# A hybrid encoder block on one core: each engine's order drawn by the other timing model

## The chip, the core and the metric

The kernel runs on one core of a Trainium2 chip. The core has five engines, each of which works off its own list of instructions in the order in which the list is written: PE (TensorE, matmuls, with PEld for its weight loads), DVE (VectorE), ACT (ScalarE), POOL (GpSimd) and SP (SyncE, which here does nothing but issue transfers). An instruction that needs another engine's or a transfer's result carries a wait, and while it waits everything behind it in its list waits too. The metric is the device time of one execution in microseconds (us).

## The reference

The reference is one layer of an encoder with 2048 tokens of width 1024, in float32. What it computes, cut to its core:

```python
xn = rmsnorm(h, norm_mix_g)
q, k, v, u, y = split(xn @ w_in)              # 3 x 512 attention, 2 x 512 recurrence
q, k = rope(q), rope(k)
attn = dilated_mixture_attention(q, k, v)     # 8 heads x 64, three (window, dilation) patterns, merged by lse
uc = centred_depthwise_conv(u, conv_w, conv_b)
rec = bidirectional_rglru(uc, gates...) * gelu(y)   # forward and backward linear recurrence
h = h + concat([attn, rec]) @ w_out
h = h + memory_cross_attention(rmsnorm(h), rmsnorm(mem))    # 4 heads x 128, 256 memory tokens
h = h + square(relu(rmsnorm(h) @ w_mlp_in)) @ w_mlp_out     # hidden width 4096
return rmsnorm(h, norm_final_g)
```

## The kernel before

Every product of the large matrices is made in three matmuls (`mm3`, lines 120 to 123): each operand is split into a high part, rounded by ACT (a copy into a rounded type), and a low part, the difference, made by DVE or POOL. So behind every load stands an ACT instruction and a subtraction, and the matmuls wait for those.

The work runs in stages that follow one another in time:

- 0 to about 700 us: the combined input projection, unit by unit (`block`, line 582). For a unit the raw weights come through a ring of three buffers (`wraw`, line 232: load, line 233; high part on ACT, line 234; low part on POOL or DVE, line 235). The products land in a rotation of matmul banks and are finished by kind: u and y (`uy_unit`), v (`v_unit`, line 458 scales the product and frees the bank), q and k (`qk_unit`, which calls `rope`, lines 378 to 395: six DVE instructions, then the high part at 392, the low part at 393 and their stores at 394 and 395, each from one of two buffers). Beside the projections a generator (`lru`, line 470) runs the recurrence in 16 chunks of 512 tokens by 128 channels, one step of it after each piece of projection. A chunk has a convolution (`conv`, lines 496 to 501) and for both directions two gate matmuls into the two banks named "a" (lines 519 and 522), which ACT reads and frees with a tanh (lines 520 and 523); then further functions on ACT (lines 524 to 526, the square root at 533) and scans on DVE (lines 538 and 543). ACT loads a function table where the next function isn't in the present one.
- at about 700 us a seam: the last q unit, and the first head's loads (`load_head`, line 178), among them the v tiles (lines 193 to 202) on SP's queue.
- 760 to about 1200 us: the attention, in units of two tiles with scores, transposes and values written two units apart (line 866 on), the recurrence's half of the output projection as filler.
- 1200 to about 1700 us: the other half of the output projection and the cross-attention.
- 1700 to about 2230 us: the MLP's first product (`InPair`, line 1131), 32 passes of seven products of block sums and differences.
- 2230 us to the end: the second product (`Part`, line 1259, and the loop at 1437), 16 passes of seven products; its sums and differences (lines 1257, 1282 to 1294) and its low parts (line 1305) are shared between DVE and POOL, and DVE adds each product to the accumulators (line 1459).

Nearly all transfers are issued by SP, from one queue, in the order of its list; POOL issues the loads of q and k.

What sets the order. The Python code is not the order of the lists. It is run once and writes down the instructions; the framework then plans them. It keeps a clock for every engine and a model of what each instruction and each transfer takes, and at each moment an engine takes, among the instructions whose inputs the model says are there, the one with the earliest place in the written order. The order in which the plan takes them is the engine's list. Tiles that share a ring get their buffers in the same pass. The written order is moved by hand in a few places: `tc.high_priority` (lines 628 and 1365) gives a stretch an earlier place, and `tc.issue_after` (lines 639, 666, 868, 1400) puts instructions behind a named one whatever the plan says. These hold under either model. The waits that keep the result right are worked out from the data, not from the plan's times, so the times decide only the order.

## Time and profile before

| what | value |
|---|---|
| median of 3 runs | 2923.38 us (2919.47 to 2930.01) |
| the profiled execution's own time | 2928.47 us |
| its span, first to last instruction | 2926.6 us |
| mean granted clock of PE | 0.942 |
| busy: PE, DVE, ACT, POOL | 2590.2, 2010.9, 1277.1, 1256.2 us |
| moved by transfers | 372.00 MB, 127 GB/s over the span |

The profile is of one execution. A busy time is the time in which an engine runs an instruction; in the rows of groups and of the order of time, what stands in brackets or behind the last bar is the idle time of the engine just before, and what ended it. "PE m L121 <- DVE v L458" reads: PE's matmul of line 121 into a bank named m waited until DVE's instruction of line 458 had run on a tile named v. SPq is SP's queue of issues. PEclk is the share of full speed that the throttle granted to PE.

### The profile page before, as it was taken

Reading aid. Unit: us, or ns where it says so; the run is one execution under the profiler, and the core shown is the slowest. Engines: PE = TensorE matmul, PEld = TensorE weight load, DVE = VectorE, ACT = ScalarE, POOL = GpSimd, SP = SyncE. Lnnn points to the kernel's source line nnn. Section 1 sums busy time; section 2 is a strip of 40 time slices with the busy share of each in tenths; the row PEclk is TensorE's granted clock in tenths of the full one; section 3 lists DMA queues with packets and bytes.
Section 4 is the critical chain, followed back from the end, with each engine's and each line's share of the span. In section 5 each row is a group of like instructions: output and inputs, shape, how many; then the busy total and the mean of one; then the engine's idle time right before and its main releaser. Section 6 shows DMA issues by size and latency. Waiting matters only on the chain. (4 is left out here: it accounts for less than half of the span.)

```text
span 2926.6 us, 39992 instructions
## 1 busy us (share of the span) xinstructions
PE 2590.2 (89%) x14074; PEld 2196.7 (75%) x14074; DVE 2010.9 (69%) x3361; ACT 1277.1 (44%) x2349; POOL 1256.2 (43%) x888
## 2 busy tenths in 40 slices
PE   7897776776779989897997899989999999999997
PEld 6776665665679989786885788868887777778776
DVE  6644656765678878634567754474447999999997
ACT  5527355461646656623444233343333333334342
POOL 2222120203334434343124655555655776666652
PEclk9998888888789999898998999999999999999999
DMA  7452334426667876554344433343336222122213
GB/s 194 144 133 82 105 81 145 123 96 156 180 170 189 216 181 155 187 160 123 101 136 142 143 109 112 109 140 112 112 108 216 86 73 87 65 87 80 72 58 115
DMA packets 267352, 372.00 MB, mean 127 GB/s; under 512 B 93072, under 2 KB 139792, under 8 KB 264080
## 3 DMA queue, kind: packets, MB, share of 16 engines
q1 hardware_dynamic: 262864, 342.19, 38.3%
q0 software_dynamic: 4288, 27.27, 4.0%
q8 instruction: 111, 1.82, 0.3%
q14 instruction: 89, 0.73, 0.1%
HBM read 254.73 MB, written 114.65 MB: 126 GB/s over the span
## 5 line engine op out<-in xcount | busy, mean ns | idle before, releaser
L1304 ACT ACTIVATE c<-raw 128x512 fp32r<-128x512 f32 x162 | 102.2, 632 | 272.2 <-PE m L122 147.5
L1155 POOL TENSOR_TENSOR wl<-wr,wh 128x512 fp32r<-128x512 f32 x96 | 145.4, 1515 | 150.2 <-ACT wh L1154 150.1
L1154 ACT ACTIVATE wh<-wr 128x512 fp32r<-128x512 f32 x128 | 80.9, 632 | 287.4 <-PE m L122 153.9
L763 ACT ACTIVATE sm<-sm,obp 128x256 f32<-128x256 f32 (+1 forms) x384 | 161.9, 468 | 48.1 <-DVE obp L760 41.4
L1155 DVE TENSOR_TENSOR wl<-ws,wh 128x512 fp32r<-128x512 f32 x96 | 81.0, 843 | 130.0 <-ACT wh L1154 124.7
L235 POOL TENSOR_TENSOR wl<-wraw,wh 128x512 fp32r<-128x512 f32 x48 | 71.0, 1484 | 198.0 <-ACT wh L234 195.5
L760 DVE CUSTOM_DVE_ANT_0 sm<-a,msk 128x256 f32<-128x256 f32 (+1 forms) x384 | 131.2, 371 | 31.9 <-PE a L757 28.2
L121 PE MATMUL m<-xh,wh 128*128 128x512 f32 x328 | 132.6, 404 | 19.6 <-ACT xh L329 8.1
L775 ACT ACTIVATE ph<-b 128x512 f16<-128x512 f32 (+1 forms) x192 | 100.4, 523 | 94.1 <-PE b L772 88.6
L1176 DVE TENSOR_TENSOR c<-m,c 128x512 f32<-128x512 f32 x64 | 44.2, 690 | 139.9 <-PE m L123 137.9
L776 DVE SCALAR_TENSOR_TENSOR pl<-b,ph 128x512 f16<-128x512 f32 (+1 forms) x192 | 114.6, 598 | 26.5 <-ACT ph L775 22.7
L122 PE MATMUL m<-xl,wh 128*128 128x512 f32 x328 | 131.8, 402 | 0.3 <-DVE xl L330 0.3
L772 PE MATMUL b<-prt,sm 128*128 128x128 f32 x640 | 108.5, 285 | 26.2 <-DVE pl L776 17.2
L123 PE MATMUL m<-xh,wl 128*128 128x512 f32 x328 | 130.9, 399 | 0.0
L1305 POOL TENSOR_TENSOR wh<-raw,c 128x512 fp32r<-128x512 f32 x58 | 93.6, 1631 | 78.1 <-ACT c L1304 66.1
L702 POOL TENSOR_SCALAR kc<-kh 128x1024 fp32r<-128x1024 f32 x32 | 68.6, 2144 | 129.6 <-PE a L756 117.4
L756 PE MATMUL a<-kc,qb 128*128 128x256 f32 x256 | 108.7, 425 | 6.0 <-DVE obp L760 5.9
L1177 DVE SCALAR_TENSOR_TENSOR c<-c 128x512 f32<-128x512 f32 x96 | 111.6, 1163 | 1.0
L234 ACT ACTIVATE wh<-wraw 128x512 fp32r<-128x512 f32 x96 | 57.8, 623 | 118.2 <-DMA wraw<-in_w_in 70.0
L1154 ACT ACTIVATE wh<-ws 128x512 fp32r<-128x512 f32 x96 | 60.5, 630 | 109.6 <-PE m L122 107.9
L123 PE MATMUL m<-t3h,wl 128*128 128x512 f32 x276 | 107.6, 390 | 0.4 <-POOL wl L1155 0.3
L121 PE MATMUL m<-wh,xh 128*128 128x256 f32 x192 | 62.1, 328 | 51.3 <-DVE v L458 33.9
(556 smaller groups left out, 9789.6 us busy)
## 6 DMA issues: line engine op xcount, KB each, us to landing
wr<-in_w_m SPq DMA_DIRECT2D x64, 512.0 KB
hid_d<-c SPq DMA_DIRECT2D x128, 256.0 KB
wraw<-in_w_in SPq DMA_DIRECT2D x80, 256.0 KB
raw<-in_w_m SPq DMA_DIRECT2D x33, 512.0 KB
rawt<-hid_d SPq DMA_DIRECT2D x26, 512.0 KB
t0h<-hid_d SPq DMA_DIRECT2D x26, 512.0 KB
o_d<-obp SPq DMA_DIRECT2D x16, 528.0 KB
obr<-o_d SPq DMA_DIRECT2D x16, 528.0 KB
```

The source lines that it names most:

```text
L121: pe.matmul(o, ah, bh, start=start, stop=False, **kw)
L122: pe.matmul(o, ah, bl, start=False, stop=False, **kw)
L123: pe.matmul(o, al, bh, start=False, stop=stop, **kw)
L756: pe.matmul(so, q0, kh[:, w0:w0 + 256], start=True, stop=False)
L760: dve.tensor_tensor_reduce(out=sm, in0=sps[:, 256 * z + o0:256 * z + o0 + kw], in1=msk[:, m:m + kw], op0=ALU.add, op1=ALU.min, scale=1.0, ...
L763: exps.append(act.activation(sm, sm, AF.Exp, scale=-1.0, bias=self.obp[:, oc, 65:66]))
L772: pe.transpose(pt[:, c0:c0 + 128], self.sm[:, z, 128 * g:128 * g + 128], idt)
L776: dve.scalar_tensor_tensor(self.pl[:, :w], pt[:, :w], 1024.0, self.ph[:, :w], op0=ALU.mult, op1=ALU.subtract)
L1154: act.activation(h, self.a[n], AF.Copy)
L1155: last[n % 2] = (pool if n % 2 else dve).tensor_tensor(l, self.a[n], f32(h), op=ALU.subtract).ins
L1177: dve.scalar_tensor_tensor(z, z if n < 6 else o, 0.0, z, op0=ALU.max, op1=ALU.mult)
L1304: act.activation(h[-1], tk, AF.Copy)
```

## The change

One argument is given to the framework's context. Its planner works as before, by the same rule and from the same written order, but takes its times from its other timing model, the one that follows each transfer event by event (the issue, the queue, the transfer on its engines, the notice of its end) rather than pricing it as a whole. No line that computes, loads or stores is touched.

```diff
-    with tile.TileContext(nc) as tc:
+    with tile.TileContext(nc, schedule_with_timeline_sim=True) as tc:
         hybrid_block(tc, *args)
```

## The prediction

> **What bounds the kernel now.** I read the page first, then the busy time in eight stretches that follow the kernel's parts, then the waits of PE stretch by stretch, and last the order of time around the longest waits. The forecast is made against the profiled execution, whose span is 2926.6 us and whose own time is 2928.47 us (1.9 us lie around the span). That is 5.1 us above the median of the runs, 2923.38 us.
>
> ```profile
> span 2926.6 us, 39992 instructions
> ...
> PE 2590.2 (89%) x14074; PEld 2196.7 (75%) x14074; DVE 2010.9 (69%) x3361; ACT 1277.1 (44%) x2349; POOL 1256.2 (43%) x888
> ```
>
> ```profile
> core 0: us, PE busy (x) PEld busy (x) DVE busy (x) ACT busy (x) POOL busy (x), PEclk, DMA share, GB/s
> 0.00:300.00 300.00, 253.00 (x1218) 211.53 (x1218) 159.54 (x253) 151.81 (x244) 67.08 (x76) 0.93 0.50 139
> 300.00:700.00 400.00, 305.35 (x1490) 258.67 (x1489) 261.98 (x336) 190.73 (x276) 73.23 (x70) 0.86 0.40 111
> 700.00:760.00 60.00, 19.17 (x113) 16.83 (x112) 26.00 (x58) 13.17 (x24) 7.16 (x8) 0.63 0.65 179
> 760.00:1200.00 440.00, 397.60 (x4021) 387.54 (x4020) 346.09 (x1201) 275.45 (x694) 176.86 (x119) 0.94 0.69 179
> ...
> 1700.00:2230.00 530.00, 519.88 (x2276) 428.37 (x2275) 284.03 (x332) 188.60 (x332) 302.72 (x198) 0.99 0.34 117
> 2230.00:2927.00 697.00, 650.51 (x2907) 529.81 (x2906) 641.95 (x726) 267.77 (x382) 429.21 (x239) 0.99 0.27 92
> ```
>
> The reader is to see three different kernels here. From 1700 to 2230 us (the MLP's first product) PE is busy 519.88 of 530 us at a granted clock of 0.99: there is nothing to win, and DVE (284 us) and ACT (189 us) have so much slack that a different order of theirs costs nothing either. From 2230 us on (the second product) PE and DVE are both nearly full, 651 and 642 of 697 us. And from 0 to 760 us (projections and recurrence) PE stands idle for 760 − 253.00 − 305.35 − 19.17 = 182 us, at a clock down to 0.86 and 0.63. That is where order can matter most. The waits of PE there, 300 to 700 us:
>
> ```profile
> PE a L121 <- ACT tr L520: 42.6, 5, 11.8
> PE m L121 <- DVE v L458: 24.8, 7, 7.0
> PE m L121 <- ACT wh L234: 17.4, 2, 9.3
> PE a L121 <- ACT ti L523: 8.1, 3, 4.0
> ```
>
> The first and the last are the gate matmuls of the recurrence: 42.6 + 8.1 = 50.7 us. They need one of the two "a" banks, which ACT frees by its tanh (lines 520, 523). What ACT did at the longest of them, in order of time (the rows of ACT, then PE's):
>
> ```profile
> 344.84 0.63 ACT L234 ACTIVATE wh<-wraw 128x512 fp32r<-128x512 f32 x1 [13.03 <-DMA wraw<-in_w_in]
> 345.49 1.28 ACT L520 ACT_TABLE_LOAD   x1
> 346.78 0.69 ACT L520 ACTIVATE tr<-a,gbh 128x512 f32<-128x512 f32 x1
> ...
> 483.95 0.72 ACT L329 ACTIVATE xh<-xr,prt 128x512 fp32r<-128x512 f32 x1 [9.38 <-DMA xr<-in_xT]
> 484.57 0.67 ACT L520 ACTIVATE tr<-a,gbh 128x512 f32<-128x512 f32 x1
> ```
>
> ```profile
> 347.52 0.80 PE L121 MATMUL a<-uh,gh 128*128 128x512 f32 x1 [10.97 <-ACT tr L520]
> ...
> 485.30 0.79 PE L121 MATMUL a<-uh,gh 128*128 128x512 f32 x1 [6.02 <-ACT tr L520]
> ...
> 512.61 0.80 PE L121 MATMUL a<-uh,gh 128*128 128x512 f32 x1 [11.76 <-ACT tr L520]
> ```
>
> ACT stood 13.03 and 9.38 us before an instruction whose load had not landed, and the tanh that PE wanted was the next one in its list and was run as soon as ACT was past it. An engine works off its list in the order written there, so a load that lands later than the planner believed holds up whatever is listed behind its reader. The plan had the load landed by then; on the chip it was not.
>
> **The change, part by part.** No instruction is added or removed: the 14074 matmuls, 3361 DVE and 2349 ACT instructions stay, with the same tiles and the same bytes. What moves is the order in each list: at each moment of the plan an engine takes, among the instructions whose inputs the plan has ready, the earliest written one, and the plan's moments now come from a model that follows each transfer.
>
> *Gate waits, 300 to 700 us.* If the plan knows that the weights land late, it lists the tanh ahead of the split that waits for them. Of the waits quoted, 10.97 and 6.02 us are plainly of this kind (17 us); at 512.61 a wait for a load is only part. Bounds: 0 (the new model has the loads land as early as the old) and 50.7 us (all such waits go). I take half, −25 us, since 17 are shown and part of the 11.76 is alike.
>
> *The clock behind those waits.* The matmul after a wait takes 0.80 us in the rows above. The stretch ran at a mean clock of 0.86, the attention stretch, with fewer waits, at 0.94. If half the gate waits go and the clock rises to 0.89, the 305.35 us of work become 305.35 × 0.86 / 0.89 = 295: −10 us. Bounds: 0, and 305.35 × (1 − 0.86 / 0.94) = 26 us.
>
> *What is late next.* The ring of raw weights has three buffers, filled by SP and emptied by ACT's split (line 234) and the subtraction behind it on POOL or DVE (line 235):
>
> ```profile
> SPq L233 <- POOL wl L235: 33.5, 11, 7.4
> ```
>
> SP issues the next load only when a buffer is read out (33.5 us of waits, 11 times). A split that is listed later, behind the tanh, frees its buffer later, and SP's queue, on which every other load and store of this stretch stands behind that wait, issues later. PE waited twice for finished weights, 17.4 us together; I count one more such wait, 17.4 / 2 = +9 us. Bounds: 0, and one for each of the six longest gate waits, 6 × 8.7 = 52 us.
>
> *The waits for v.* (24.8 us) PE has all matmul banks full there; only an earlier DVE instruction helps, and the plan prices DVE much the same. I take 0; bounds −12 (half) and +12.
>
> *The seam to attention, 700 to 760 us.* PE waits 31.15 us there for the last rotary pair:
>
> ```profile
> 705.59 5.52 SPq L194 DMA_DIRECT2D v<-v_d  x1
> ...
> 712.46 6.50 SPq L394 DMA_DIRECT2D k_d<-rh  x1
> 719.05 7.23 SPq L395 DMA_DIRECT2D k_d<-rl  x1
> ```
>
> ```profile
> 732.00 0.69 DVE L393 SCALAR_TENSOR_TENSOR rl<-t,rh 128x512 fp32r<-128x512 f32 x1 [17.97 <-DMA k_d<-rl]
> ...
> 739.12 0.58 PE L756 MATMUL a<-kh,qb 128*128 128x256 f32 x1 [31.15 <-DVE t L385]
> ```
>
> SP's issues of one load and two stores took 5.52 + 6.50 + 7.23 = 19 us, and DVE waited 17.97 us for a store to give its buffer back. The v load was issued before those stores were ready, and a planner that takes what is ready will issue it first again. I take 0; bounds −18 (DVE's wait goes) and +10.
>
> *Attention (760 to 1200) and what lies between.* PE is at 398 of 440 us. 0, bounds ±10.
>
> *The second MLP product.* The planner's order there can differ only in how far ahead DVE and POOL split. 0; the bound follows with the rival that it makes.
>
> Sum: −25 − 10 + 9 = −26 us, so 2928.5 − 26 = 2902.5 for a profiled run, and **2897 us** on the median's scale (2923.4 − 26).
>
> **The rivals.** *DVE beside POOL (slower).* In the second product, 13 passes of 40 us; DVE's busy time on line 1305, then on line 1257, then two forms of line 1305 (min/median/max ns):
>
> ```profile
> 2270.00:2790.00 520.00, 235.91 (x142) 203.64 (x128) 1.00 0.24 80
> ...
> 2270.00:2790.00 520.00, 45.36 (x26) 126.25 (x46) 1.00 0.24 80
> ```
>
> ```profile
> L1305 DVE TENSOR_TENSOR wh<-raw,c x23: 675/691/1357, 2252.0 to 2767.5; 128x512 fp32r<-128x512 f32 x23
> ...
> L1305 DVE TENSOR_TENSOR t1l<-t1h,t1l x8: 1209/2434/2831, 2277.6 to 2787.0; 128x1024 fp32r<-128x1024 f32 x8
> ```
>
> The same subtraction takes 1209 ns or 2831 ns, by what runs beside it; POOL is busy over 60% of this stretch. A pass now has (235.91 + 45.36) / 13 = 21.6 us of such work on DVE. If the redrawn order puts all of it beside POOL, nine of 1024 elements at 2434 ns and four of 512 at 1357 ns give 27.3 us, 5.7 more. DVE's spare time is (697 − 641.95) / 16 = 3.4 us a pass; from that point on the pass grows: 5.7 − 3.4 = 2.3 us, times 16 passes +37 us. Without the gain ahead of it that is 2960 us. For it: DVE is already what PE waits for there. Against it: a lucky overlap is as likely as an unlucky one, and the bound the other way is the same size. The Trainium skill (GPSIMD Engine Reference, section 1, Specifications) says that POOL shares its SBUF interfaces with VectorE and that an instruction of DVE with two SBUF inputs contends for them; lines 1305 and 1257 are of that kind, and the trace agrees, 1209 against 2831 ns.
>
> *Waits change places (no difference).* Each gate wait that goes is followed by a wait for weights, since the ring is paced by how long a load takes: −50.7 + 52, the clock as it was, 2923 us. The same time results if the change doesn't do what it says, because the two models agree on the order wherever it matters.
>
> *A recurrence that comes late (slower).* Passing the waiting readers lets projections run ahead of the recurrence, and its rest is run at the seam, with PE at the 0.63 clock and 19 of 60 us busy. Its 16 chunks fill at least the 400 us from 300 to 700, 25 us a chunk; left over at the seam, a chunk has nothing beside it. From about one chunk on this outweighs the gain; for two, 2897 + 2 × 25 = 2947 us. For it: PE's list would then hold fewer gates in a stretch where they are what it waits for. Against it: the recurrence is written ahead of the projections that it runs beside, and so comes first whenever it is ready.
>
> ```profile
> L533 ACT ACT_TABLE_LOAD x13 | 16.7, 1283 | 0.2
> ```
>
> A new order of ACT also draws the table loads anew: ten more would be 13 us of ACT at the row's 1283 ns, in a stretch (300 to 700) where ACT is busy 191 of 400 us, so I leave them out. The Trainium skill (ScalarE: Activation LUTs, section What ACT_TABLE_LOAD costs) prices a switch at about 2.66 us with the drain; by it ten more would be 27 us, an estimate, where the trace shows 1.29 us from a load's start (345.49) to the next instruction's (346.78).
>
> **How the numbers follow.** The forecast has 0.50, waits that change places 0.15, DVE beside POOL 0.18, the late recurrence 0.17. A measurement of this kernel can tell about 0.3%, 9 us. Faster 0.50, same 0.15, slower 0.35. The forecast's own range goes from −60 (gate waits and clock at two thirds of their bounds, 51, and 9 us from the rest) to −9: 2863 to 2914 us. The range for the time reaches 15 us further down, for the seam's 18, and up past both slower rivals, with the larger one grown by a half (2923 + 56): 2848 to 2980 us.
>
> **What would show it.** Right: ACT's waits for the raw weights and for x shrink and no tanh stands behind them; gate waits from 300 to 700 us fall from 51 to about 25 us, the clock there rises to 0.89, the stretch ends 25 us sooner, and everything from 1700 us on keeps its length. Wrong: PE's waits for finished weights take their place; the second product's passes leave 40 us; or the seam grows. If the time lies over 2932 us, the idea that the plan's early loads were the fault is wrong, or its gain was lost in the second product.

## The result, and the profile after

The changed kernel takes 3012.84 us (median of 4 runs, 3003.89 to 3026.26) against 2923.89 us for the kernel before on the same chip: the ratio is 1.0317, 95% interval 1.0289 to 1.0346. It is 3.2% **slower**. The forecast was 2897 us, and the range ended at 2980: wrong in sign and outside the range. The profiled execution took 3003.89 us, its span is 3002.1, 75.5 us more than before.

The head of the page of the changed kernel (PE's busy time, share of the span and instructions, then the other engines):

```profile
span 3002.1 us, 40037 instructions
...
PE 2613.6 (87%) x14074; PEld 2216.9 (74%) x14074; DVE 1984.8 (66%) x3361; ACT 1283.7 (43%) x2354; POOL 1281.4 (43%) x888
```

The work is the same: 14074 matmuls, 3361 DVE and 888 POOL instructions (ACT has 5 more, table loads). Of the 75.5 us, PE is busy 23.4 longer (2613.6 − 2590.2) with the same matmuls, and idle 52.1 longer.

For a fair comparison I cut both traces at the same work rather than at the same times: at the first instruction of a line that opens a stage (756 the first scores, 923 the other half of the output projection, 1171 the MLP's first product, 1459 the second, 1483 the end). The busy time in those stretches, before:

```profile
0.00:739.10 739.10, 566.33 (x2740) 476.46 (x2740) 435.82 (x607) 345.06 (x524) 147.47 (x153) 0.88 0.46 126
739.10:1204.40 465.30, 408.80 (x4096) 398.11 (x4096) 362.19 (x1257) 287.63 (x715) 178.61 (x121) 0.92 0.68 180
1204.40:1607.40 403.00, 360.87 (x1720) 296.50 (x1720) 221.07 (x374) 161.67 (x353) 136.77 (x144) 0.94 0.47 141
1607.40:2250.80 643.40, 620.25 (x2675) 508.32 (x2676) 370.61 (x415) 221.62 (x388) 379.11 (x240) 0.98 0.36 123
2250.80:2868.10 617.30, 591.35 (x2577) 479.68 (x2575) 579.12 (x636) 244.77 (x338) 400.10 (x212) 1.00 0.25 84
2868.10:2926.60 58.50, 42.62 (x269) 37.68 (x268) 42.07 (x77) 16.33 (x34) 14.12 (x19) 0.89 0.36 126
```

And of the changed kernel:

```profile
0.00:786.20 786.20, 576.91 (x2740) 485.95 (x2740) 430.20 (x609) 355.12 (x529) 155.14 (x153) 0.85 0.41 119
786.20:1269.40 483.20, 420.07 (x4097) 406.24 (x4097) 350.32 (x1240) 285.72 (x713) 180.17 (x119) 0.90 0.65 174
1269.40:1690.50 421.10, 365.85 (x1725) 298.11 (x1721) 214.91 (x378) 159.47 (x350) 135.98 (x144) 0.93 0.42 133
1690.50:2345.30 654.80, 624.49 (x2677) 508.41 (x2678) 379.53 (x427) 224.70 (x391) 370.09 (x241) 0.97 0.36 123
2345.30:2937.50 592.20, 580.57 (x2556) 478.04 (x2555) 560.12 (x629) 241.13 (x338) 422.62 (x210) 1.00 0.25 84
2937.50:3002.10 64.60, 45.72 (x289) 40.11 (x287) 49.70 (x86) 17.56 (x37) 17.43 (x23) 0.87 0.37 131
```

The matmuls of a stretch agree to within 5, but for the last two: 21 fewer in the second product, 20 more in the tail behind it. At 0.23 us a matmul some 5 us of the second product's 25.1 have only moved across that cut.

The reader is to see that the loss isn't in one place. The first stage grows by 47.1 us, attention by 17.9, the middle by 18.1, the first product by 11.4; the second product *shrinks* by 25.1 and the tail grows by 6.1. In each stage that grows the granted clock is 0.01 to 0.03 lower, and the same matmuls take longer (566.33 to 576.91 us for 2740 of them in the first stage): where PE stands idle longer, its matmuls also run at a lower clock. The Trainium skill (TensorE: Matmul & The Clock Gate, section HAM oscillation) says that idle gaps of PE over some 3.4 us bring the throttle back; the rows agree in the direction, and no row here shows that threshold.

PE's waits of the changed kernel from 300 to 700 us, the stretch that the prediction argued from:

```profile
PE m L121 <- ACT wh L234: 35.0, 3, 15.8
PE a L121 <- ACT tr L520: 18.7, 5, 7.5
PE a L121 <- ACT ti L523: 18.4, 5, 5.2
PE m L121 <- DVE t L385: 17.1, 2, 14.4
PE b L121 <- DVE t L386: 11.9, 1, 11.9
PE m L121 <- DVE v L458: 7.2, 3, 4.7
PE b L121 <- DVE v L458: 5.0, 1, 5.0
PE b L121 <- DVE t L385: 3.0, 1, 3.0
```

```profile
300.00:700.00 400.00, 283.49 (x1348) 239.40 (x1347) 254.65 (x328) 202.61 (x283) 70.75 (x66) 0.82 0.37 106
```

The gate waits did fall (50.7 to 18.7 + 18.4 = 37.1 us) and so did those for v (26.3 to 12.2; the prediction's row has 24.8 of the 26.3, the bank named b has the rest), but the waits for finished weights doubled (17.4 to 35.0), and 32.0 us of waits for the banks that the rotary step reads (17.1 + 11.9 + 3.0, lines 385 and 386) stand where there were none. In the same 400 us PE did 1348 matmuls instead of 1490.

### The profile page after: what moved, and what is told of

Same layout as the page of the kernel before. It is cut to its first block, busy times and chain, and to the rows that moved or that the text cites. A ratio compares the mean times of both kernels' runs of the same rounds, so it can differ in the third digit from the quotient of the medians.

```text
span 3002.1 us, 40037 instructions
## 1 busy us (share of the span) xinstructions
PE 2613.6 (87%) x14074; PEld 2216.9 (74%) x14074; DVE 1984.8 (66%) x3361; ACT 1283.7 (43%) x2354; POOL 1281.4 (43%) x888
## 4 chain that ended last, share of the span: by engine, by line
PE 55%; DMA 19%; DVE 15%; ACT 5%; issue 4%; POOL 2%; SPq 0%; DVEq 0%; ACTq 0%; POOLq 0%
PE m L121 13%; PE m L122 13%; PE m L123 13%; DMA obr<-o_d 3%; DMA k_d<-rl 2%; PE a L123 2%; PE a L121 2%; PE a L122 2%; DMA h_d<-h 2%; PE a L756 2%; DMA wraw<-in_w_in 2%; DMA q_d<-rl 1%; PE b L772 1%; PE b L122 1%; PE b L123 1%
## 5 line engine op out<-in xcount | busy, mean ns | idle before, releaser
L1155 POOL TENSOR_TENSOR wl<-wr,wh 128x512 fp32r<-128x512 f32 x96 | 132.3, 1379 | 168.0 <-ACT wh L1154 168.0
L1155 DVE TENSOR_TENSOR wl<-ws,wh 128x512 fp32r<-128x512 f32 x96 | 97.2, 1014 | 116.3 <-ACT wh L1154 99.5
L760 DVE CUSTOM_DVE_ANT_0 sm<-a,msk 128x256 f32<-128x256 f32 (+1 forms) x384 | 129.5, 374 | 66.8 <-PE b L772 64.1
L121 PE MATMUL m<-xh,wh 128*128 128x512 f32 x328 | 134.8, 412 | 41.6 <-DVE t L385 17.1
L756 PE MATMUL a<-kc,qb 128*128 128x256 f32 x256 | 112.7, 440 | 23.6 <-DVE obp L760 23.4
L1154 ACT ACTIVATE wh<-ws 128x512 fp32r<-128x512 f32 x96 | 60.6, 631 | 117.1 <-PE m L122 115.1
L1305 POOL TENSOR_TENSOR wl<-raw,c 128x512 fp32r<-128x512 f32 x58 | 101.3, 1760 | 19.7 <-ACT c L1304 19.7
L121 PEld LDWEIGHTS m<-xh,wh 128*128 128x128 f32 x328 | 65.1, 199 | 58.3 <-issue 15.5
```

Of the source, the lines that this page charges most:

```text
L121: pe.matmul(o, ah, bh, start=start, stop=False, **kw)
L756: pe.matmul(so, q0, kh[:, w0:w0 + 256], start=True, stop=False)
L760: dve.tensor_tensor_reduce(out=sm, in0=sps[:, 256 * z + o0:256 * z + o0 + kw], in1=msk[:, m:m + kw], op0=ALU.add, op1=ALU.min, scale=1.0, ...
L1154: act.activation(h, self.a[n], AF.Copy)
L1155: last[n % 2] = (pool if n % 2 else dve).tensor_tensor(l, self.a[n], f32(h), op=ALU.subtract).ins
L1305: self.eng[n].tensor_tensor(l[-1], tk, f32(h[-1]), op=ALU.subtract)
```

## The experiments

Most kernels here keep one program and change only what the planner may do. A *pinned* list is a list of instruction names in a fixed order, held by dependencies between neighbours that order the plan and put no wait on the chip:

```diff
     with tile.TileContext(nc) as tc:
         hybrid_block(tc, *args)
+        _pin(tc, _PINS)
...
+def _pin(tc, orders):
...
+        for a, b in zip(names, names[1:]):
+            tc.add_manual_dep(ins[b], a, info, reason="pin")
```

All ratios are to the kernel before, timed on the same chip, with their 95% intervals.

**Is it the lists alone?** The new model is on, and all five lists are pinned to those of before.

> The other timing model is on, but every engine's list is pinned, instruction by instruction, to the list of the kernel before. Theory 'lists': the model acts only through the order, so this runs at the time of before, 2924 us (within 0.3%). Rival 'buffers': the model also hands out the ring buffers differently and the loss lies there: above 2950 us although the lists are those of before.

Measured: 1.0008 (0.9985 to 1.0031). The model acts through the order and nothing else that the time shows. It is also the yardstick for the traces: with the same lists, its five stages took 744.1, 455.5, 407.0, 645.0 and 614.9 us, up to 10 us from those of before, so a single stage's difference below 10 us isn't read.

**Which stage?** The old lists (all engines pinned), with one stage's instructions, on all engines, in the order of the changed kernel. First the stage up to attention:

> The model of before, all lists pinned: those of before, but for the instructions of the projections and the recurrence (all that is written ahead of attention) in the order of after. Theory 'first stage': the loss is made there, since attention's first matmul started 47 us later in the trace of after; 2924 + 47 = 2971 us. Rival 'seam': the 47 us only show up there and come from later stages' instructions listed among the projections; then below 2940 us.

Then attention:

> The model of before, lists of before, but for the instructions of the attention stage in the order of after, on all engines. In the trace of after this stage took 483 us against 465 before (first score matmul to first transpose of the output projection). Theory 'own order': its 18 us come from its own order, 2924 + 18 = 2942 us. Rival 'handed on': the loss comes from how the stage before ends (late stores at the seam), and does not come with the order: within 0.3% of before.

The output projection with cross-attention, and the first MLP product, together:

> The old lists, with the output projection and cross attention and the first MLP product in the changed order. In the changed kernel these stages were 18.1 and 11.4 us longer. If the lists of these stages make that themselves: +25 to +30 us, ratio 1.008 to 1.011. If it was carried over from ahead (loads, the clock): within 0.3% of before, 2915 to 2932 us.

And the second MLP product:

> The model of before, lists of before, but for the instructions of the second MLP product in the order of after. In the trace of after this stage (first to last accumulation of line 1459's kind) was 25 us shorter. Theory 'last stage gains by its order': 2924 - 25 = 2899 us. Rival 'phase': the gain came from how DVE and POOL happened to meet after the earlier stages, and does not follow the order: 2915 to 2935 us.

| stage in the changed order | ratio (95%) | that stage's length: before, changed kernel, here (us) |
|---|---|---|
| up to attention | 1.0191 (1.0144 to 1.0237) | 739.1, 786.2, 790.0 |
| attention | 1.0102 (1.0069 to 1.0135) | 465.3, 483.2, 482.7 |
| output projection and cross-attention | 1.0130 (1.0096 to 1.0165), both | 403.0, 421.1, 423.5 |
| first MLP product | the same run | 643.4, 654.8, 662.5 |
| second MLP product | 0.9966 (0.9942 to 0.9990) | 617.3, 592.2, 596.3 |

The busy rows of the transplanted stages, of the first, the attention, the middle and the last run in turn:

```profile
0.00:790.00 790.00, 573.02 (x2740) 482.24 (x2740) 430.74 (x609) 355.37 (x529) 157.04 (x153) 0.85 0.42 118
```

```profile
744.50:1227.20 482.70, 417.80 (x4097) 403.90 (x4097) 352.07 (x1242) 285.51 (x713) 180.27 (x119) 0.91 0.67 174
```

```profile
1200.30:1623.80 423.50, 368.35 (x1720) 299.38 (x1720) 213.50 (x362) 158.77 (x347) 133.27 (x143) 0.93 0.43 134
1623.80:2286.30 662.50, 624.06 (x2678) 507.04 (x2679) 379.10 (x428) 225.60 (x393) 371.32 (x241) 0.97 0.36 120
```

```profile
2253.40:2849.70 596.30, 583.47 (x2557) 479.29 (x2557) 561.28 (x628) 240.70 (x337) 419.99 (x210) 1.00 0.26 85
```

Each stage takes nearly the length that it has in the changed kernel as soon as it has its lists, though the stages ahead of it have the old ones, and to 0.01 even its clock. So each stage's loss, or gain, is made in the main by its own order. The sum isn't exact: the five lengths add up to +86.9 us here and to +69.4 in the changed kernel, and the four ratios to 3.9% against 3.2%. I had expected less of the attention run than it cost (its span is 29.7 us longer, of which 17.4 lie in the stage), less of the two middle stages (1.008 to 1.011), and more of the last run: 25 us, where the medians differ by 14. There the stage is 21.0 us shorter and the tail behind it 6.1 longer (64.6 us), as in the changed kernel.

One seam carries something over. With attention's old lists and another first stage ahead, attention took from 450.9 us (the run on the first 170 us below) to 480.1 us (the run with three buffers below), so the moment of the first score is a soft mark. Up to the end of attention, both stages together, the run with the first stage's lists is 44.9 us longer than before, that with attention's lists 22.8, and the changed kernel 65.0, so these two do add up.

**What is it in attention?** PE's longest waits there from 760 us on, of before:

```profile
PE b L772 <- DVE pl L776: 17.2, 11, 7.2
...
PE a L756 <- DVE obp L760: 5.9, 2, 4.3
```

The same in the run with only attention's lists changed:

```profile
PE a L756 <- DVE obp L760: 25.3, 14, 6.6
PE b L772 <- DVE pl L776: 9.8, 5, 7.5
```

Over the whole stage, its start included, the wait for line 760 is 15.6 us before and 35.0 in this run. The changed kernel has 23.4 us, 13 times, in the first of these rows. In PE's list of before 15 of the 192 score units follow another score unit without a transpose in between; in the new one 50 do. Units in a row need their "a" banks sooner, and those are what DVE is still reading (line 760). The waits of the transposes get shorter in return. PE's idle time grows from 56.5 to 64.9 us, and its busy time by 9.0 at a lower clock. That the bunching makes the wait is read from the rows; no run took the bunching alone.

**When in the first stage?** The plan's first 1000 instructions (some 170 us, ahead of the recurrence) in the changed order, then the old; and the complement.

> The old model's lists, with the first 1000 instructions of the plan (589 of PE, 95 of SP, some 170 us on the chip, before the recurrence begins) in the changed order. Loads theory: memory's and positions' loads stand between the loads of x, the first finished unit is 14 us late, and the lag is carried to the end: +14, 2937 us, ratio 1.005. Rotary theory (the loss of the first stage arises from 300 us on, when the projections wait for rotary tiles and these for their stores): the lag of the head is made up again in the recurrence's stretch and the ratio is 1.000 to 1.002.

> The complement: the old lists for the first 1000 instructions of the plan, then the changed order to the end of the first stage, then the old lists. The whole first stage in the changed order was +56 us (ratio 1.019). Loads theory: +40 is left (56 less 14), ratio 1.014. Rotary theory: all of it is left, +50 to +56, ratio 1.017 to 1.019. If the head alone sets where the recurrence starts and so the rest: +20 or less, ratio under 1.008.

Measured: 1.0043 (1.0022 to 1.0065) and 1.0103 (1.0072 to 1.0134), so about 12.4 and 33 us between the medians (the whole first stage: 51). The second lies between what the theories asked for. The early part agrees with the theory of the loads. SP's issues near the start, before, then in the changed kernel:

```profile
10.11 0.33 SPq L233 DMA_DIRECT2D wraw<-in_w_in  x1
10.48 7.52 SPq L324 DMA_DIRECT2D xr<-in_xT  x5
...
21.38 1.37 SPq L279 DMA_DIRECT2D mraw<-in_memT  x3
```

```profile
7.84 1.30 SPq L279 DMA_DIRECT2D mraw<-in_memT  x2
10.75 0.33 SPq L364 DMA_DIRECT2D n<-in_pos  x1
12.19 0.33 SPq L324 DMA_DIRECT2D xr<-in_xT  x1
...
23.14 2.10 SPq L279 DMA_DIRECT2D mraw<-in_memT  x2
25.34 0.58 SPq L324 DMA_DIRECT2D xr<-in_xT  x1
```

Loads of the memory and the positions, needed much later, stand between the loads of x that the first products need; the recurrence's first tanh comes at 241.6 us in this run, at 225.4 before and at 235.9 in the changed kernel. That run changes the head on every engine, so the loads are the likely cause and not an isolated one. Nor does its profiled execution, one of its faster ones, show where the 12.4 us stay: its first score comes 16.7 us later than before, and its attention ends 2.3 us later. The complement puts the rest of the loss into one stretch. From 225 to 500 us it does as many matmuls as before; from 500 to the first score it needs 274.5 us instead of 239.1 for about the same number (here the two halves of that run):

```profile
225.00:500.00 275.00, 210.00 (x1013) 176.48 (x1011) 164.50 (x210) 161.35 (x225) 52.63 (x52) 0.88 0.32 93
500.00:775.00 275.00, 166.03 (x823) 141.01 (x822) 152.05 (x203) 98.26 (x138) 44.42 (x40) 0.79 0.42 118
```

PE waits there for the rotary step's lines 385 and 386, 61.6 us (before, 31.2 in the same stretch):

```profile
PE a L756 <- DVE t L385: 28.1, 1, 28.1
...
PE m L121 <- DVE t L385: 18.4, 2, 14.6
...
PE b L121 <- DVE t L386: 11.3, 1, 11.3
...
PE b L121 <- DVE t L385: 3.8, 1, 3.8
```

In the changed kernel and here the recurrence is used up early (its last tanh pair begins at 630.8 and 616.7 us; before, 655.3), the last projections run without it, and the rotary results wait for their stores to give the buffers of rh and rl back (DVE for rl's, from 500 to 810 us: 58.6 us here, 43.9 before). The next four runs try these two causes.

**Is it the early recurrence?** First by holding it back: the new model on, and 16 dependencies that keep the later gate matmuls behind the projections that they followed before.

```diff
+        _hold(tc, _HOLD)
...
+    for a, b in pairs:
+        tc.add_manual_dep(ins[f"I-{b}"], f"I-{a}", info, reason="hold")
```

> The new model draws all lists, but the last 83 of the recurrence's 192 matmuls may not stand ahead of the projection matmuls behind which they stood before (16 holds). In PE's list of the first stage (2718 matmuls) the recurrence then ends at place 2525, against 2285 in the changed kernel and 2453 before. Theory 1, the loss comes from PE using the recurrence up early and running the last projections alone: the first score matmul comes at 745 to 760 us instead of 786, and the time is 2975 to 2990 us, ratio 1.017 to 1.024. Theory 2, the rotary chain and its stores are late in the other lists and PE's places only show it: 775 to 795 us, 1.028 to 1.036. Theory 3, holding one engine's places makes the lists fit each other worse, as capping and single lists did: over 1.036.

Measured: 1.0376 (1.0344 to 1.0409), the first score matmul at 808.3 us. But the holds did more than was meant: the last tanh pair begins at 720.8 us, 65 later than before. So this run shows that a recurrence held back so far is no cure for the new lists, and not that its early end is innocent. Then from the other side, the old model with the recurrence written at a faster and at a slower pace:

```diff
-                due[0] += 1.3
+                due[0] += 1.4     # the other run: 1.2
```

> The old model, with the pace at which the recurrence is written among the projections raised from 1.3 to 1.4 steps. In PE's list the recurrence then ends at place 2341 of 2718 (before: 2453, changed kernel: 2285); the stages from the output projection on keep PE's lists as they were. Theory 1 (a recurrence used up early leaves projections alone): +15 to +35 us in the first stage, ratio 1.005 to 1.012. Theory of fit (it isn't the place of the recurrence, but that the new model's lists of the first stage are a worse plan as a whole): within 0.4% of before.

> The same with 1.2 steps: the recurrence ends at place 2621 of 2718. Theory 1: no loss, or a gain of up to 10 us, ratio 0.996 to 1.002, unless its rest is left at the seam (the prediction's late recurrence: 25 us a chunk, ratio 1.008). Theory of the lucky draw (the order of before is a good one among many, any redrawing costs): 1.005 to 1.02 here and in the run beside it, whichever way the recurrence goes.

Measured: 0.9978 (0.9954 to 1.0002) and 1.0028 (1.0003 to 1.0053). With the early recurrence the first score matmul comes at 723.9 us, 15 *ahead* of before, and the stretch from 500 us on is 15.2 us shorter at a clock of 0.85 (0.84 before):

```profile
500.00:723.90 223.90, 168.10 (x828) 142.46 (x828) 149.79 (x194) 100.21 (x143) 42.64 (x36) 0.85 0.45 124
```

So a recurrence that ends earlier costs nothing in the old plan, as far as this run goes: its last tanh pair begins at 642.0 us, 13 earlier than before, where it is 25 in the changed kernel and 39 in the run that loses from 500 us on. The explanation that I had read out of the changed trace asked for 15 to 35 us here and got none; for a still earlier end it isn't tested. Redrawing the first stage by the old model changed the time by 0.3% at most in these two runs, less than the lucky draw asked for: two draws of that model are about as good as the order of before.

**Is it the stores of the rotary results?** The lists that lose from 170 us on, with a third buffer for rl (there is no room for a third one for rh as well).

```diff
-                l = p2.tile([P, 512], F32R, tag="rl", name="rl", bufs=2)
+                l = p2.tile([P, 512], F32R, tag="rl", name="rl", bufs=3)
...
-                        "ss": lambda: p2.tile([P, 512], F32, tag="rl", name="vss", bufs=2),
+                        "ss": lambda: p2.tile([P, 512], F32, tag="rl", name="vss", bufs=3),
```

> The lists of the run in which the first stage after 170 us stands in the changed order (ratio 1.0103, first score matmul at 774.5 us), with three buffers for the remainder rl in place of two. There DVE waited 32.4 + 26.2 = 58.6 us from 500 to 810 us for a store to give rl back, and PE 28.1 + 18.4 + 11.3 + 3.8 = 61.6 us from 500 to 775 us for rotary tiles. Theory 2 (the stores hold the rotary chain up): first score matmul at 735 to 755 us, ratio 0.997 to 1.003. Theory 1 (the projections run alone; the chain is as long without the wait, since ACT waits 54.0 us for the same stores to give rh back): 765 to 775 us, ratio 1.007 to 1.011.

Measured: 1.0121 (1.0091 to 1.0151), no gain on 1.0103. DVE's and ACT's waits there from 500 to 800 us:

```profile
DVE rl L393 <- ACT rh L392: 29.3, 3, 15.2
...
DVE rl L393 <- DMA k_d<-rl: 10.5, 4, 4.0
DVE rl L393 <- DMA q_d<-rl: 8.0, 2, 4.3
```

```profile
ACT rh L392 <- DMA q_d<-rh: 40.5, 4, 19.5
...
ACT rh L392 <- DMA k_d<-rh: 20.1, 6, 7.1
```

The wait for rl's store shrank from 58.6 to 18.5 us, and DVE now waits 29.3 us for ACT's high part, which waits 60.6 us for *its* buffer. The first score matmul could start at 757.6 us instead of 774.5, but the next then waited 24.8 us (PE a L756 <- DVE obp L760). The ratio is theory 1's, or a little above it, for a reason that neither theory named, and theory 1 found no support in the runs before this. One of two rings that wait for stores of the same kind was widened, so the stores are not cleared of the loss; the twin was not tried.

**Is it one engine's list?** The new model on, with one list (or two) pinned to before, or the reverse:

> The other timing model is on and plans ACT, DVE, POOL and SP; only PE's list is pinned to that of before. Theory 'PE': the loss is made by PE's own list, which after has moved most (matmuls of two product groups alternate, and projections run behind the recurrence); then close to before, 2900 to 2935 us. Rival 'feeders': the loss is in the lists of the engines that feed PE (ACT, DVE, SP), and stays: 2980 to 3020 us.

> The other timing model is on; only SP's list, which issues nearly all transfers, is pinned to that of before. Theory 'issue order': after, SP's list issues transfers for later work (the memory's and the positions' loads) between the loads that PE is about to need, PE starts the first unit 14 us late, and so on through the first stage; with SP's list of before most of the loss goes: 2925 to 2960 us. Rival 'compute lists': the loss is in ACT's and DVE's order and stays: 2985 to 3020 us.

> The model of before plans ACT, DVE, POOL and PE; only SP's list is pinned to that of after. The reverse of the run above. Theory 'issue order': most of the loss comes with SP's list, 2975 to 3020 us. Rival 'compute lists': 2920 to 2950 us.

> The other timing model is on; ACT's and DVE's lists are pinned to those of before, and SP, POOL and PE are planned by the model. Theory 'issue order': SP's list is still the model's and the loss stays above 2970 us. Rival 'compute lists': ACT and DVE, once listed as before, take the loss away, 2920 to 2945 us.

| lists | ratio (95%) |
|---|---|
| new, PE's of before | 1.0305 (1.0249 to 1.0361) |
| new, SP's of before | 1.0399 (1.0357 to 1.0440) |
| old, SP's of the changed kernel | 1.0845 (1.0798 to 1.0893) |
| new, ACT's and DVE's of before | 1.0688 (1.0653 to 1.0722) |

None of these lists carries the loss, and neither the order of SP's issues nor the lists of ACT and DVE account for it, as the two theories of these runs had it. Against the changed kernel's 1.0317, PE's old list changes nothing, SP's old list adds 0.8% and ACT's and DVE's 3.6%; the new list of SP in the old plan costs 8.5%. Lists belong together: the better plan's list is no help to the other engines' lists of the worse one. POOL's list wasn't tried, nor ACT's and DVE's singly.

**Is it running ahead?** In the new lists PE stands further ahead of the written order. Both models, with a cap:

```diff
+        _window(tc, {'PE': 24})
...
+        for a, b in zip(l, l[w:]):     # l: the engine's instructions in written order
+            tc.add_manual_dep(b, a.name, info, reason="window")
```

> The new model draws all lists, but no PE instruction may stand ahead of one written more than 24 PE instructions before it. In the changed kernel PE ran up to 157 (projections and recurrence) and 219 (attention) instructions ahead, 24.8 and 73.2 in the mean; here 1.0 and 4.3, close to what it was before. Theory A, running ahead is the fault (the recurrence is used up early, attention falls out of its order): the two first stages get back to about 740 and 465 us and the time lies between 2905 and 2945 us, ratio 0.995 to 1.007. Rival B, it isn't PE's running ahead but where loads, rotary work and stores stand in the other lists: the time stays at 1.02 to 1.04, 2980 to 3040 us, with PE waiting for the same rotary tiles.

> The old model with the same cap of 24 on PE. Before, PE ran 7.4 instructions ahead in the mean in the first stage (at most 93) and 1.8 in attention. Theory A says that less of it never hurts: 2895 to 2925 us, ratio 0.99 to 1.0. Rival B, the old order's running ahead is what fills PE while rotary tiles are late: the first stage grows by some 10 to 30 us, ratio 1.003 to 1.01. Rival C, any redrawing of the lists lands somewhere between 0.99 and 1.04, whatever the cap: no order between this run and the one beside it.

Measured: 1.0479 (1.0449 to 1.0508) and 1.0117 (1.0077 to 1.0156). Theory A falls under both models. Under the old one the first stage grew to 763.1 us, which fits rival B: there the running ahead fills PE.

**A version that beats both.** The old lists, the second MLP product in the new order, three buffers for rl.

> The old lists with the second MLP product in the changed order (ratio 0.9966 when it was run by itself), and three buffers for rl. Before, DVE waited 36.5 + 7.4 = 43.9 us from 500 to 810 us for stores to give rl back, 18.0 of it ahead of the first score matmul. Theory 2: the seam loses most of those 18 us, ratio 0.989 to 0.993, 2890 to 2903 us. Theory 1: the list is as it was and the chain ends on something else, ratio 0.995 to 0.998.

Measured: 0.9946 (0.9922 to 0.9971), 2915.69 us beside 2930.69 for before. The profiled second product took 594.6 us, as in the changed kernel; the first stage, at 740.1 us, gained nothing from the buffer. So the win is the last stage's order, and the buffer's part can't be told from nothing (0.9966 without it). Why that order is better shows in PE's waits inside the passes, 520 us of before, then of the changed kernel:

```profile
PE m L121 <- DVE wr L1459: 10.0, 6, 1.7
PE m L121 <- DVE t6l L1459: 5.7, 6, 1.0
PE a L121 <- DVE t6l L1459: 3.3, 5, 0.7
```

```profile
PE m L121 <- DVE t6l L1459: 10.8, 6, 1.9
```

PE's waits for the accumulating line 1459 fall by half, and its idle time in the stage from 26.0 to 11.6 us. DVE is busy 19.0 us less there (579.1 to 560.1, with 7 instructions fewer), POOL 22.5 us more (400.1 to 422.6, with 2 fewer). With the tail, where some of DVE's work has gone, it is 11.4 us less for DVE and 25.8 more for POOL, with 2 instructions more on each. So the price of working side by side seems to have moved from DVE to POOL: of the last one, one kind of subtraction on line 1305 (`c<-raw,ws`) went from a median of 1302 ns to 2276. PE waits less for DVE and hardly for POOL (0.2 us). That is read from the rows; no run took it alone.

## Why the prediction was wrong

*Gate waits (−25).* The mechanism is there, the size was not: 50.7 to 37.1 us, so −13.6.

*The clock behind them (−10).* Wrong sign: 0.86 to 0.82 from 300 to 700 us. All of PE's idle time there rose from 94.7 to 116.5 us while the gate waits fell; I had let the clock follow that one kind of wait.

*What is late next (+9).* One more wait for finished weights came, as written, but of 17.6 us (17.4 to 35.0). This step also failed in kind: it looked for the next late thing in the ring of weights alone. 32.0 us of waits for the rotary step between 300 and 700 us were in no term.

*The waits for v (0, bounds ±12).* 26.3 to 12.2 with both banks: just past the bound, on the good side, with nothing in the sum for it.

*The seam (0).* The wait for the last rotary pair went from 31.15 to 27.6 us; the loss lies ahead of it, in the waits for the earlier pairs.

*Attention and what lies between (0, bounds ±10).* **This is a step that failed.** Their own lists cost +17.4 and +20.5 us. The bound had no row behind it: that PE was busy 398 of 440 us was taken to mean that an order can't lose much, but 50 score units in place of 15 could be put behind one another, and the wait for line 760 went from 15.6 to 35.4 us over the stage.

*The first product ("nothing to win", a different order costs nothing).* +11.4 us (+19.1 with its lists alone). Slack of DVE and ACT says what a better order can't win; it doesn't say that a worse one is free.

*The second product (0).* −25.1 us in the stage, some 5 of them moved into the tail. The rival "DVE beside POOL" had put a price of up to +37 us on a new draw there and noted that the bound the other way was as large; it came out on that other side. *A recurrence that comes late*: it came 25 us earlier, and the earlier one that was tried cost nothing. *Waits change places* was right for the weights only.

The step that failed under all of these was the premise. I took a fault that the old plan plainly has (readers of loads ahead of tanhs) for the measure of the new plan, and priced everywhere else at zero. But the planner redraws all lists: two thirds of PE's instructions stand at another place. The last sentence of the prediction left two readings of a time over 2932 us. The gain was not lost in the second product, which got shorter; what remains is that "the idea that the plan's early loads were the fault is wrong" as an account of what the change does.

What is shown: the change acts through the order alone; each stage's own lists make its loss or gain; the loss of the first stage comes in part with the order of its first 170 us (12.4 us) and more with the rest (33), where it arises from 500 us on; it is not in PE's or SP's list alone, nor in those of ACT and DVE together, and not in PE's running ahead. An early recurrence as its cause is unlikely, not excluded. What stays open: why the event-following model's plan is worse in four stages and better in one. The stores that hold rh and rl, and the order of the early loads, were each tried only in part.

## What to carry to other kernels

A switch of the planner's timing model is a new draw of every list at once: price it stage by stage, with a bound for a worse draw in stages that look safe, not only by the faults that the old plan shows. The lists of a plan belong together, so compare and combine plans by stage, all engines at once; one engine's list from another plan won nothing here, and cost up to 8.5%. Pinning costs no time by itself (1.0008), and by stage it found the one stage (596.3 against 617.3 us) worth taking from a change that loses 3.2%.

## What the runs showed that I had not expected

- A third of the added time is not idle time: PE's busy time grew by 23.4 of 75.5 us for the same 14074 matmuls, as the mean clock fell from 0.942 to 0.925.
- A third buffer moved a wait to its twin: DVE's 58.6 us for rl's stores became 18.5, and 29.3 for ACT's rh appeared, which waits for stores of the same kind.
- The first score matmul is a poor milestone: it came 15 us ahead of before with the early recurrence, and the whole kernel gained 0.2%, with an interval that reaches 1.0002. With three buffers it came 17 us ahead of the same lists with two, and attention took 480.1 us in place of 454.3.
